# A two-layer hybrid backbone in float32: the second layer's output projection by eight plain pairs of blocks, in place of seven combined products, under a new table of ranks

## The chip, the cores and the metric

The kernel runs on one core of a Trainium2 chip. TensorE (PE) multiplies matrices, VectorE (DVE), ScalarE (ACT) and GpSimd (POOL) work element by element, and SyncE (SP) issues the DMAs. The metric is the device time of one launch in microseconds; the time quoted is the median of three runs.

## The reference

Latent tokens `x` (1024 tokens of width 1024) and context tokens (256 of the same width) pass through two layers. In float32, each layer does:

```python
hx = rms_norm(x, g_mix[i]) * (1.0 + sc1) + sh1
zx = hx @ w_in[i]                                  # 1024 -> 1280 columns: q, k, v, pool, fourier
mx = jnp.concatenate([latent_attention(q, k, v, kc, vc),       # 512 columns
                      pool_mix(...), fourier_mix(...)], -1)    # 256 + 256 columns
x = x + ga1 * (mx @ w_out[i])                      # the output projection, 1024 x 1024
fx = rms_norm(x, g_ffn[i]) * (1.0 + sc2) + sh2
x = x + ga2 * swiglu(fx, w_gate_up[i], w_down[i])  # 1024 -> 2 x 2816 -> 1024
```

The context goes through the same steps in the first layer. In the second layer it only gives keys and values, and `x` alone is returned.

## The kernel before, in words

Everything is kept transposed: features on the 128 partitions, tokens along the free axis. The latent tokens are two chunks, A (token offset 256, 512 tokens) and B (offset 768, 512 tokens); a width of 1024 is eight blocks of 128 features, called k as an input and ct as an output.

A float32 product is made of three matmuls. Each operand is written as a high part, rounded to the format that TensorE takes at full rate, and a low part, the rest: one cast (`hi`) and one subtraction (`lo`), in `halve` (L1730). `mm3` (L483) then issues low by high, high by low and high by high, on L485, L486 and L487. So one 128x128 block of weights times 512 tokens is three matmuls of 128x512.

The output projection of both chunks is a 2 by 2 by 2 block product: w_out in four quarters of 512x512, and the mixers' output in four tiles (chunk A or B, k 0 to 3 or k 4 to 7; k 0 to 3 are the attention's heads, k 4 to 7 the pool and Fourier parts). Before, it is done by seven combined products (Strassen's scheme, table `SEVEN`). Each product has 4 output blocks of 4 inputs, times 3 matmuls. Its two operands are sums or differences of quarters and of tiles: `block` (L1854) loads a half row of a quarter and the operation named `out sum` adds two of them; `summed` (L1742) adds two tiles of the mixers' output into a scratch page `ws` (`mix sum`). Both are then split by `halve` (`out hi`, `out lo`, `mix hi`, `mix lo`). Each finished accumulator `ps_o` is added to `x`, scaled, by `add_to` (L1879), in one or two places: 12 places times 4 blocks, 48 additions (named `residual`, L1883). The products come in the order 5, 7, 1, 2, 4, 3, 6; chunk A is complete after the fifth, chunk B after the seventh.

`finish_x` (L1868) then stores the chunk and runs its norm (`normed`, L1758): squares on ACT, their sums on DVE, a matmul that adds over partitions (L699), root, reciprocal, a matmul that spreads the result (L708), eight scalings on DVE (L1765), eight shifts on ACT, and the operands of the next combined products: A0 and DA from chunk A alone; B1, DB, S1, S7, S6 with chunk B.

In the second layer the FFN starts with five early units (`EARLIES`, L376), each a pair of products that needs only A0 and DA; then come units that need DB and B1, S1, S7 and S6. FFN weights may be loaded only once `second_pass` has begun, the first matmul of the seventh product (L1917).

SBUF is cut into named pages of 4 KB per partition (`H`, `W`, `MIX`, `RES`, `C`, `ST`). The attention uses `H[768][:4]`, `H[256][:4]`, `C`, `RES[0]` and `b6` for its softmax pages; the page `ws` is taken from `C[2:]` after the attention's last value products.

No instruction order is written out by hand. Each piece of work is an operation of a `Plan` with its cost, its predecessors, the pages and PSUM banks it takes, and a rank. `Plan.run` simulates the engines and issues, at each step, the ready operation that can start first, by rank among those close together. The rank is the place in the program plus an entry of `SHIFTS` by name and layer; the entries reach some 4 ms either way, so they act as priorities. `ENGINES` says for each name which of ACT (A), DVE (D) and POOL (G) may do it, and the planner chooses among them. TensorE's own products stay in program order. Names in the attention: `Z` scales a softmax page of 1024 columns, `Y` one of 256, `C` copies transposed blocks out of PSUM, `O` copies a finished head out of PSUM.

The few lines that order the projection:

```python
Y_ORDER, Y_FINAL = (5, 7, 1, 2, 4, 3, 6), {256: 4, 768: 6}
...
        for n, p in enumerate(Y_ORDER):
            blocks, how, to = SEVEN[p]
            for two in (0, 2):
...
                    e = seven(dst, w, yop[p], [AREAS] * (q == two), gate if n == 0 and q < 2 else ())
```

Of the kernel before, what the change touches and what calls it, by code (L numbers as in the profile page):

```python
# [13 lines left out]
ALU = mybir.AluOpType  # L14
# [5 lines left out]
KT = D_MODEL // P  # L20
# [256 lines left out]
def setting(table, name, default):  # L277
# [13 lines left out]
ENGINES = {"C": "AD", "G": "G", "H": "ADG", "O": "A", "Y": "AD", "Z": "ADG", "act hi": "A", "act lo": "DG", "act sum": "D",  # L291
# [6 lines left out]
           "mix sum": "DG", "norm hi": "ADG", "norm lo": "G", "norm shift": "ADG", "out hi": "A", "out lo": "DG",  # L298
# [4 lines left out]

SHIFTS = ({"C": 919100, "EC": -545700, "EL": -1073100, "MC": -4100900, "ML": 314500, "N": -759500, "O": -2444400,
           "R": -2036600, "SA": 235500, "SB": -740400, "SC": -579700, "T": -221600, "V": -416700, "Y": 278400,
           "Z": 895000, "aa": -841600, "act hi": -1263600, "act lo": -1492900, "act sum": 1970600, "ada": -662600,
# [65 lines left out]

Y_ORDER, Y_FINAL = (5, 7, 1, 2, 4, 3, 6), {256: 4, 768: 6}
Y_RANK, LEAD_Y = 0, 20000
CT_GATE = 5
EARLIES = (2, 2), (5, 0)  # L376

STARTS = (((0, 0), (0, 1), (1, 0), (1, 1)), ((0, None), (1, None)))
# [2118 lines left out]
```

## Time and profile before

| what | us |
|---|---|
| median of 3 runs (2601.51 to 2606.92) | 2603.08 |
| the profiled execution, its own time | 2608.01 |
| its span | 2605.9 |
| TensorE busy in the span | 2531.5 |
| VectorE busy | 2091.2 |
| ScalarE busy | 1253.5 |
| GpSimd busy | 540.2 |

A busy TensorE is counted from the start of a matmul to a modelled end, and matmuls overlap: the time between two starts is shorter than one matmul's duration. "Idle before, releaser" tells how long an engine waited and which instruction ended the wait. The second layer's projection lies at about 1860 to 1952 us of the span, the first layer's at 480 to 620.

### The profile page before, as it was taken

The page shows a single profiled execution, that of the slowest core. Times are in us where ns is not written, and L with a number is a line of the kernel's source. Part 1 is how long each engine was busy: PE and PEld are TensorE (multiplying, and loading weights), DVE is VectorE, ACT ScalarE, POOL GpSimd, SP SyncE. Part 2 cuts the span into 40 slices and gives each one's busy share as a digit, 9 for nine tenths or more (in the row PEclk, how much of TensorE's full clock was granted, in tenths as well). Part 3 has the DMA queues.
Part 4 walks back from the last instruction along what each step waited for, and adds up shares of the span by engine and source line. Part 5 has one row for each costly group of instructions (what it writes and reads, how often), then busy time and mean ns, then how long its engine had stood idle before and what let it go on. Part 6 is the DMA issues. An engine that isn't in the chain of part 4 may idle for free.

```text
span 2605.9 us, 38612 instructions
## 1 busy us (share of the span) xinstructions
PE 2531.5 (97%) x14382; PEld 2092.5 (80%) x14382; DVE 2091.2 (80%) x3466; ACT 1253.5 (48%) x2319; POOL 540.2 (21%) x450
## 2 busy tenths in 40 slices
PE   6999999998999999999999999999998999999999
PEld 5887777787788888888888988777776888888887
DVE  6766877799866998876788987877799977777886
ACT  4324888746322222224444533899746333334442
POOL 2022222122200000000223313322132311111241
PEclk9999999999999999999999999999998999999999
DMA  8243200354224455448434333100352423225733
GB/s 296 84 130 109 75 1 1 114 182 131 96 91 146 154 164 169 145 156 291 148 97 125 105 93 101 39 1 1 99 183 87 158 107 115 81 98 213 231 95 124
DMA packets 126203, 314.83 MB, mean 121 GB/s; under 512 B 14784, under 2 KB 23360, under 8 KB 126016
## 3 DMA queue, kind: packets, MB, share of 16 engines
q1 hardware_dynamic: 126016, 312.36, 36.4%
q8 instruction: 114, 1.87, 0.3%
q14 instruction: 73, 0.60, 0.1%
HBM read 244.94 MB, written 62.13 MB: 118 GB/s over the span
## 4 chain that ended last, share of the span: by engine, by line
PE 78%; DVE 14%; ACT 3%; DMA 2%; issue 2%; POOL 0%; SPq 0%; DVEq 0%; ACTq 0%; POOLq 0%
PE ps_s L485 8%; PE ps_s L486 8%; PE ps_s L487 8%; PE ps_d L485 6%; PE ps_d L486 6%; PE ps_d L487 6%; PE ps_pv L1512 5%; PE ps_t L1488 4%; PE ps_s L1537 4%; DVE half L475 3%; PE ps_in L485 3%; PE ps_in L486 3%; PE ps_in L487 3%; DVE x L1883 2%; DVE ws L475 1%
## 5 line engine op out<-in xcount | busy, mean ns | idle before, releaser
L472 ACT CAST half<-ws 128x512 fp32r<-128x512 f32 x404 | 243.9, 620 | 524.0 <-PE ps_s L487 236.6
L486 PE MATMUL ps_s<-half 128*128 128x512 f32 x1056 | 413.8, 392 | 6.4 <-DVE half L475 6.4
L485 PE MATMUL ps_s<-half 128*128 128x512 f32 x1056 | 414.8, 393 | 3.2 <-ACT half L472 2.6
L487 PE MATMUL ps_s<-half 128*128 128x512 f32 x1056 | 412.5, 391 | 0.0
L485 PE MATMUL ps_d<-half 128*128 128x512 f32 (+1 forms) x792 | 290.7, 367 | 2.0 <-ACT half L472 2.0
L486 PE MATMUL ps_d<-half 128*128 128x512 f32 (+1 forms) x792 | 290.2, 366 | 0.5 <-DVE half L475 0.5
L487 PE MATMUL ps_d<-half 128*128 128x512 f32 (+1 forms) x792 | 290.1, 366 | 0.0
L475 DVE TENSOR_TENSOR half<-ws,half 128x512 fp32r<-128x512 f32 x354 | 243.2, 706 | 56.6 <-ACT half L472 55.2
L486 PEld LDWEIGHTS ps_s<-half 128*128 128x128 f32 x1056 | 199.4, 189 | 50.7 <-DVE half L475 9.0
L485 PEld LDWEIGHTS ps_s<-half 128*128 128x128 f32 x1056 | 199.2, 189 | 46.6 <-ACT half L472 3.4
L487 PEld LDWEIGHTS ps_s<-half 128*128 128x128 f32 x1056 | 199.4, 189 | 41.6
L472 ACT CAST half<-wst 128x512 fp32r<-128x512 f32 x224 | 132.6, 618 | 163.9 <-PE ps_s L487 82.8
L475 POOL TENSOR_TENSOR ws<-wst 128x512 f32<-128x512 f32 x72 | 107.2, 1489 | 500.2 <-DVE half L475 413.8
L475 DVE TENSOR_TENSOR ws<-wst 128x512 f32<-128x512 f32 x258 | 173.4, 689 | 9.6 <-DMA wst<-in_w_gate_up 4.9
L475 DVE TENSOR_TENSOR half<-wst,half 128x512 fp32r<-128x512 f32 x204 | 152.3, 770 | 35.8 <-ACT half L472 35.6
L485 PEld LDWEIGHTS ps_d<-half 128*128 128x128 f32 x792 | 150.1, 190 | 26.7 <-ACT half L472 2.4
L486 PEld LDWEIGHTS ps_d<-half 128*128 128x128 f32 x792 | 150.1, 190 | 24.8 <-DVE half L475 0.7
L475 POOL TENSOR_TENSOR half<-ws,half 128x512 fp32r<-128x512 f32 x56 | 76.5, 1365 | 449.8 <-ACT half L472 396.2
L487 PEld LDWEIGHTS ps_d<-half 128*128 128x128 f32 x792 | 150.0, 189 | 24.0
L1450 DVE TENSOR_REDUCE smalls<-ps_s 128x1 f32<-128x1024 f32 x128 | 153.9, 1213 | 10.1 <-PE ps_s L1537 10.0
L485 PE MATMUL ps_in<-parts,w 128*128 128x512 f32 (+1 forms) x416 | 158.8, 382 | 1.6 <-ACT parts L472 1.6
L1512 PE MATMUL ps_pv<-pt,v 128*64 128x256 f32 x1312 | 156.4, 384 | 0.0
(284 smaller groups left out, 5874.0 us busy)
## 6 DMA issues: line engine op xcount, KB each, us to landing
wst<-in_w_gate_up SPq DMA_DIRECT2D x99, 512.0 KB, 4.3
ast<-in_w_ada SPq DMA_DIRECT2D x96, 512.0 KB, 3.7
as<-act_spill SPq DMA_DIRECT2D x165, 256.0 KB, 2.7
hs<-in_w_out SPq DMA_DIRECT2D x96, 256.0 KB, 3.0
act_spill<-c SPq DMA_DIRECT2D x44, 512.0 KB, 4.1
wst<-in_w_down SPq DMA_DIRECT2D x44, 512.0 KB, 6.4
x_spill<-x SPq DMA_DIRECT2D x28, 512.0 KB, 3.1
x<-x_spill SPq DMA_DIRECT2D x26, 512.0 KB, 6.5
```

The lines of the kernel that those rows point to most:

```text
L472: (nc.scalar.copy if e == "A" else nc.vector.tensor_copy)(out, x)
L475: (nc.vector if e == "D" else nc.gpsimd).tensor_tensor(out, x, y, op)
L485: nc.tensor.matmul(o, wl, xh, start=start, stop=False)
L486: nc.tensor.matmul(o, wh, xl, start=False, stop=False)
L487: nc.tensor.matmul(o, wh, xh, start=False, stop=stop)
L1450: nc.vector.tensor_reduce(self.pair.col(1, self.h), self.s, AX.X, ALU.max)
L1488: nc.tensor.transpose(self.t[:, 2 * q + h, :], src, ident)
L1512: nc.tensor.matmul(self.bank[own], v[:, own], self.pt[k0][:, g, 2 * P * q:2 * P * q + 2 * P], start=(k0 + q == 0), stop=(k0 + q == self.nk ...
L1537: nc.tensor.matmul(o, self.q[0][:, self.h0 + h, :], kv["k", k0](self.g, j), start=(j == 1), stop=(j == 0))
L1883: nc.vector.scalar_tensor_tensor(v, o(), s, v, ALU.mult, ALU.add)
```

## The change

The second layer alone (`DIRECT = (False, True)`) computes its projection directly. The sixteen tiles of the mixers' output (two chunks, eight k) are each split once into high and low parts, without sums. w_out is loaded by output block: eight loads of 512 KB, each split into two halves by `Feed.add` (operations `load yout`, `hi yout`, `lo yout`); the split weights stay in their pages from chunk A's use until chunk B's. The work goes by pairs of output blocks, in the order A0 A1 A2 B0 A3 B1 B2 B3 (the digit is the pair): per block eight inputs of three matmuls, k 4 to 7 first. Each accumulator is added to `x` in one place. Chunk A is complete after the fifth pair, chunk B after the eighth, and `second_pass` is the first matmul of pair B1. The first two weight blocks go into `W`; the others wait for the attention's last value products and have `W`, `c0`, `c1`, `b8`, `b9`, `a8`, `a9` and `H[0]` as rooms. The pages of the mixers' tiles (`H[256]`, `H[768]`) are freed at the last matmul of pair A3 and of pair B3.

The tables `ENGINES` and `SHIFTS` are replaced for both layers: nearly every rank differs, and many names may run on other engines. `hi yout` is not in the table and falls under `hi*`.

```diff
--- before
+++ after
-ENGINES = {"C": "AD", "G": "G", "H": "ADG", "O": "A", "Y": "AD", "Z": "ADG", "act hi": "A", "act lo": "DG", "act sum": "D",
-           "eh": "D", "el": "DG", "f copy": "AD", "gate": "DG", "hi dft": "ADG", "hi dftc": "G", "hi in0": "AG",
-           "hi in1": "ADG", "hi in2": "AD", "hi in3": "D", "hi in4": "A", "hi in5": "DG", "hi in6": "A",
-           "hi in7": "ADG", "hi in8": "AD", "hi in9": "DG", "hi out": "ADG", "hi*": "A", "k across": "DG",
-           "k hi": "ADG", "k lo": "G", "lo dft": "D", "lo dftc": "DG", "lo in0": "D", "lo in1": "D", "lo in2": "G",
-           "lo in3": "D", "lo in4": "DG", "lo in5": "G", "lo in6": "DG", "lo in7": "D", "lo in8": "DG",
-           "lo in9": "G", "lo out": "DG", "lo*": "DG", "mix copy": "A", "mix hi": "A", "mix lo": "D",
-           "mix sum": "DG", "norm hi": "ADG", "norm lo": "G", "norm shift": "ADG", "out hi": "A", "out lo": "DG",
-           "out sum": "D", "pool hi": "AD", "pool lo": "DG", "q hi": "D", "q lo": "G", "rope add": "D",
-           "rope cos": "D", "rope sin": "DG", "square": "A", "sum": "D", "u hi": "ADG", "u lo": "DG", "v copy": "A",
-           "v hi": "A", "v out": "AD", "w hi": "A", "w lo": "DG", "w sum": "DG", "x hi": "ADG", "x lo": "D",
+ENGINES = {"C": "AD", "G": "G", "H": "ADG", "O": "D", "Y": "ADG", "Z": "D", "act hi": "A", "act lo": "DG", "act sum": "D",
+           "eh": "AD", "el": "DG", "f copy": "A", "gate": "D", "hi dft": "A", "hi dftc": "ADG", "hi in0": "AD",
+           "hi in1": "G", "hi in2": "ADG", "hi in3": "AG", "hi in4": "AG", "hi in5": "AD", "hi in6": "AG",
+           "hi in7": "D", "hi in8": "ADG", "hi in9": "A", "hi out": "ADG", "hi*": "A", "k across": "A",
+           "k hi": "ADG", "k lo": "G", "lo dft": "D", "lo dftc": "DG", "lo in0": "DG", "lo in1": "G", "lo in2": "D",
+           "lo in3": "G", "lo in4": "DG", "lo in5": "G", "lo in6": "G", "lo in7": "DG", "lo in8": "D", "lo in9": "G",
+           "lo out": "DG", "lo yout": "D", "lo*": "DG", "mix copy": "A", "mix hi": "AD", "mix lo": "DG",
+           "mix sum": "DG", "norm hi": "ADG", "norm lo": "D", "norm shift": "ADG", "out hi": "A", "out lo": "DG",
+           "out sum": "DG", "pool hi": "ADG", "pool lo": "DG", "q hi": "D", "q lo": "DG", "rope add": "D",
+           "rope cos": "DG", "rope sin": "G", "square": "A", "sum": "DG", "u hi": "AG", "u lo": "DG", "v copy": "AD",
+           "v hi": "A", "v out": "AD", "w hi": "A", "w lo": "DG", "w sum": "DG", "x hi": "A", "x lo": "D",
            "x shift": "A", "x sum": "DG"}
 
 
-SHIFTS = ({"C": 919100, "EC": -545700, "EL": -1073100, "MC": -4100900, "ML": 314500, "N": -759500, "O": -2444400,
...
+SHIFTS = ({"C": 114200, "EC": -631900, "EL": -874800, "MC": -1126400, "ML": -33800, "N": -2136800, "O": 342200, "R": -480200,
...
@@ -373,6 +373,9 @@
+DIRECT = (False, True)
+Y_PAIRS = ([(256, 0), (768, 0), (256, 1), (768, 1), (256, 2), (768, 2), (256, 3), (768, 3)], [(256, 0), (256, 1), (256, 2), (768, 0), (256, 3), (768, 1), (768, 2), (768, 3)])
@@ -1807,27 +1810,36 @@
+        if DIRECT[l]:
+            for ch, h, pages in ((A, 1, H[256][4:]), (B, 1, H[768][4:]), (A, 0, H[256][:4]), (B, 0, H[768][:4])):
+                for kk in range(4):
+                    k = 4 * h + kk
+                    b = yop[ch, k] = Box()
+                    halve(b, lambda ch=ch, k=k: col(mix, ch, k), mixed(ch, k), (pages[kk],), plan.t + Y_RANK, "mix")
+                    yuse[ch, k // 2] += b.ready
+        else:
...
@@ -1837,9 +1849,10 @@
+        if not DIRECT[l]:
+            less.op = op("D", 100, negate, [mod_op[l, GA1 * KT], mod_op[l, GA1 * KT + 4]], rank=plan.t - 20000, name="negate")
...
-        for n, pages in enumerate((ST, C[:2])):
+        for n, pages in enumerate(() if DIRECT[l] else (ST, C[:2])):
@@ -1887,41 +1900,76 @@
+        if DIRECT[l]:
+            wt, room_y = {}, W + ("c0", "c1") + (("b8", "b9", "a8", "a9") + tuple(H[0]) if last else ())
+            begun_y = False
+            for ch, two in Y_PAIRS[l]:
                 o, first = Box(), None
-                for q in (two, two + 1):
-                    rank = plan.t - LEAD_Y
-                    w = Box()
-                    stage = stages[n in (2, 4, 6)]
-                    sts = [block(l, q, i_, j_, stage, rank) for i_, j_ in blocks]
-                    dep = [s.op for s in sts]
-                    if how is not None:
-                        dep = [op("sum", 512, lambda e, a=sts[0], b=sts[1], how=how: combine(e, a.t, a.t, b.t, how), dep, give=[sts[1].op],
-                                  rank=rank, name="out sum")]
-                    halve(w, lambda a=sts[0]: a.t, dep, W, rank, "out", order=[h_turn])
-                    h_turn = w.op
-                    join(w.ready, [sts[0].op])
-                    stage[2].extend(w.ready)
+                for q in range(2):
+                    ct = 2 * two + q
+                    if ct not in wt:
+                        late = len(wt) >= 2
+                        wt[ct] = feed.add(i["w_out"][l, ct], room_y if late else W, plan.t - LEAD_Y, uses["v"][0][-8:] if late else (), "yout")
+                        h_turn = wt[ct][1].op
                     def dst(*tag, o=o, q=q):
                         if tag:
                             o.t = bank(tag[0], [2, 512], "ps_o")
-                        return o.t[:, q % 2, :]
+                        return o.t[:, q, :]
                     start = len(plan.ops)
-                    e = seven(dst, w, yop[p], [AREAS] * (q == two), gate if n == 0 and q < 2 else ())
+                    e = product(dst, wt[ct], lambda k, ch=ch: [yop[ch, k].t[:, j, :] for j in range(2)],
+                                lambda k, ch=ch: yop[ch, k].ready, 512, () if begun_y else gate, [AREAS] * (q == 0),
+                                ks=(4, 5, 6, 7, 0, 1, 2, 3))
+                    begun_y = True
                     first = first or plan.ops[start]
-                    if n == 6 and q == 0:
+                    if ch == B:
+                        join([e], [h.op for h in wt[ct]])
+                    if (ch, ct) == (B, 2):
                         second_pass = first
-                    join([e], [w.op])
-                join([add_to(ch, q + 4 * z, sign, lambda o=o, q=q: o.t[:, q % 2, :], e, None)
-                      for q in (two, two + 1) for ch, z, sign in to], [first])
-            join([e], [b.op for b in yop[p]])
-            for ch in (A, B):
-                if p == Y_FINAL[ch]:
+                    a = add_to(ch, ct, 1, lambda o=o, q=q: o.t[:, q, :], e, None)
+                    added = [a] if q == 0 else added + [a]
+                join(added, [first])
+                if two == 3:
+                    join([e], [yop[ch, k].op for k in range(KT)])
                     finish_x(ch)
...
```

## Rows read from the trace of the kernel before

**Rows 1.** The profile's page: the span, and its first part, busy time of each engine with its share of the span and its instruction count.

```profile
span 2605.9 us, 38612 instructions
...
PE 2531.5 (97%) x14382; PEld 2092.5 (80%) x14382; DVE 2091.2 (80%) x3466; ACT 1253.5 (48%) x2319; POOL 540.2 (21%) x450
```

**Rows 2.** Busy time by stage. Columns: the stretch, its length, busy us (and instructions) of TensorE's matmuls, its weight loads, VectorE, ScalarE and GpSimd, the granted TensorE clock as a share of full speed, the DMA engines' share, GB/s. The stretches are the kernel's beginning, the end of the first layer's projection with the norm behind it, the attention of the second layer, and the second layer's projection and what follows it.

```profile
0.00:60.00 60.00, 38.88 (x427) 29.12 (x428) 38.21 (x70) 26.17 (x36) 12.33 (x17) 1.00 0.85 315
575.00:640.00 65.00, 54.90 (x334) 48.57 (x333) 62.95 (x112) 40.81 (x66) 19.67 (x20) 0.95 0.51 162
1630.00:1866.00 236.00, 231.06 (x1669) 178.49 (x1668) 182.79 (x363) 220.71 (x451) 59.31 (x63) 1.00 0.07 21
1866.00:1955.00 89.00, 84.59 (x387) 67.16 (x385) 83.06 (x127) 40.63 (x63) 26.42 (x19) 0.96 0.55 178
1955.00:2010.00 55.00, 44.77 (x183) 35.88 (x184) 53.97 (x87) 37.10 (x58) 8.86 (x7) 0.90 0.22 71
```

**Rows 3.** TensorE in order of time inside the second layer's projection, where it never waits: start us, duration us, instruction. These are the first and the last of 148 lines.

```profile
1905.20 0.39 PE L487 MATMUL ps_o<-half 128*128 128x512 f32 x1
...
1938.52 0.39 PE L487 MATMUL ps_o<-half 128*128 128x512 f32 x1
```

**Rows 4.** The same stretch of the second layer, from the first matmul of its projection to the last, and from there until TensorE no longer waits; columns as in rows 2.

```profile
1859.80:1952.30 92.50, 89.40 (x419) 71.90 (x418) 82.95 (x126) 42.98 (x68) 26.42 (x19) 0.96 0.51 165
1952.30:2013.00 60.70, 49.16 (x197) 38.77 (x196) 58.01 (x93) 37.65 (x58) 11.34 (x7) 0.89 0.26 82
```

**Rows 5.** The same columns for the instructions that read or write one accumulator alone: first the projection's `ps_o` in the first of these two stretches, then the FFN's `ps_s` and `ps_m` in the second.

```profile
1859.80:1952.30 92.50, 81.26 (x336) 64.32 (x336) 31.48 (x46) 0.96 0.51 165
...
1952.30:2013.00 60.70, 43.00 (x167) 33.08 (x168) 0.00 (x0) 6.01 (x6) 0.89 0.26 82
...
1952.30:2013.00 60.70, 2.88 (x12) 2.25 (x12) 0.00 (x0) 0.89 0.26 82
```

**Rows 6.** Who TensorE waited for between 1860 and 2013 us: total us, times, longest us.

```profile
PE ps_s L486 <- DVE half L475: 5.7, 5, 3.4
PE ps_ss L699 <- DVE sq L690: 4.7, 1, 4.7
PE ps_o L486 <- DVE half L475: 2.8, 2, 1.8
```

**Rows 7.** Ten microseconds of the projection after its first long wait; columns as in rows 2.

```profile
1880.00:1890.00 10.00, 7.23 (x20) 5.35 (x20) 8.93 (x15) 3.37 (x6) 0.93 (x1) 0.66 0.20 58
```

**Rows 8.** Groups of instructions between 1866 and 1955 us on VectorE, ScalarE and GpSimd: line, engine, operation, tiles, count, then busy us and mean ns of one, then the engine's idle time before them.

```profile
L1883 DVE SCALAR_TENSOR_TENSOR x<-ps_o,mod,x 128x512 f32<-128x512 f32 x40 | 27.9, 740 | 0.9 <-PE ps_o L487 0.9
...
L475 DVE TENSOR_TENSOR half<-ws,half 128x512 fp32r<-128x512 f32 x21 | 15.0, 715 | 1.5 <-ACT half L472 1.5
...
L475 DVE TENSOR_TENSOR ws<-mix 128x512 f32<-128x512 f32 x15 | 10.3, 691 | 0.5
L475 DVE TENSOR_TENSOR hs<-hs 128x512 f32<-128x512 f32 x13 | 8.9, 682 | 1.3 <-DMA hs<-in_w_out 1.3
...
L475 DVE TENSOR_TENSOR half<-hs,half 128x512 fp32r<-128x512 f32 x11 | 7.6, 689 | 0.1
...
L1883 DVE SCALAR_TENSOR_TENSOR x<-ps_o,negs,x 128x512 f32<-128x512 f32 x8 | 6.0, 744 | 0.2 <-PE ps_o L487 0.2
```

**Rows 9.** The instructions that read the mixers' output `mix`, from 1745 us on: count, shortest, median and longest ns, first and last start.

```profile
L475 DVE TENSOR_TENSOR ws<-mix x15: 683/692/693, 1869.6 to 1922.9; 128x512 f32<-128x512 f32 x15
...
L475 DVE TENSOR_TENSOR half<-mix,half x4: 678/680/684, 1766.1 to 1805.8; 128x512 fp32r<-128x512 f32 x4
```

**Rows 10.** VectorE in order of time around the two halves' norms: start us, duration us, instruction, count.

```profile
1929.17 2.71 DVE L1883 SCALAR_TENSOR_TENSOR x<-ps_o,mod,x 128x512 f32<-128x512 f32 x4
...
1944.76 1.28 DVE L1765 TENSOR_TENSOR x<-x,ps_rs 128x512 f32<-128x512 f32 x2
...
1953.01 1.40 DVE L1883 SCALAR_TENSOR_TENSOR x<-ps_o,mod,x 128x512 f32<-128x512 f32 x2
...
1957.29 2.47 DVE L1765 TENSOR_TENSOR x<-x,ps_rs 128x512 f32<-128x512 f32 x4
...
1967.16 0.68 DVE L1765 TENSOR_TENSOR x<-x,ps_rs 128x512 f32<-128x512 f32 x1
```

**Rows 11.** Groups of instructions in the second layer's attention, 1630 to 1866 us, columns as in rows 8. `p` and `pt` are the softmax's exponentials and their transposes.

```profile
L472 DVE COPY pt<-ps_t 128x512 f32<-128x512 f32 x74 | 49.8, 683 | 14.0 <-PE ps_t L1488 14.0
L472 ACT COPY pt<-ps_t 128x512 f32<-128x512 f32 x84 | 47.9, 589 | 5.3 <-PE ps_t L1488 5.1
...
L1475 POOL TENSOR_SCALAR p<-p,smalls 128x1024 f32<-128x1024 f32 x31 | 35.8, 1154 | 128.6 <-ACT pt L472 75.0 <-PE ps_s L1537 44.8 <-DVE smalls L1555 5.3
L1473 ACT ACTIVATE p<-p,smalls 128x1024 f32<-128x1024 f32 x30 | 34.3, 1144 | 0.0
...
L472 ACT COPY mix<-ps_pv 128x256 f32<-128x256 f32 x15 | 5.6, 376 | 0.0
...
L1475 DVE TENSOR_SCALAR p<-p,smalls 128x1024 f32<-128x1024 f32 x3 | 2.2, 745 | 0.0
```

**Rows 12.** The weight conversions of both layers' projections: shortest, median and longest ns of one on VectorE and on GpSimd.

```profile
L475 DVE TENSOR_TENSOR half<-hs,half x32: 672/683/1156, 279.2 to 1933.5; 128x512 fp32r<-128x512 f32 x32
L475 POOL TENSOR_TENSOR half<-hs,half x24: 1269/1300/2134, 493.5 to 1941.1; 128x512 fp32r<-128x512 f32 x24
```

**Rows 13.** The profile's sixth part, DMA issues: out<-in, queue, operation, count, KB each, median us from issue to landing.

```profile
wst<-in_w_gate_up SPq DMA_DIRECT2D x99, 512.0 KB, 4.3
```

More of the change, by code (lines that the diff above doesn't have):

```diff
@@ new lines, in layer @@
+        if DIRECT[l]:
[6 more added lines that the diff above has]
+        else:
+            YP = [(5, H[256][4:], ((B, 1),), None), (7, H[768][4:], ((A, 1), (B, 1)), ALU.add),
+                  (1, H[256][:4], ((A, 0), (B, 1)), ALU.add), (2, H[768][:4], ((A, 0),), None),
+                  (4, H[256][4:], ((A, 1), (A, 0)), ALU.subtract), (3, H[768][4:], ((B, 0), (B, 1)), ALU.subtract),
+                  (6, H[256][:4], ((A, 0), (B, 0)), ALU.add)]
+            y_turn = None
+            for p, pages, tiles, how in YP:
+                yop[p] = [Box() for _ in range(4)]
+                for kk in range(4):
+                    ts = [(ch, 4 * h + kk) for ch, h in tiles]
+                    src_ = [lambda ch=ch, k=k: col(mix, ch, k) for ch, k in ts]
+                    deps = [d for ch, k in ts for d in mixed(ch, k)]
+                    if how is None:
+                        halve(yop[p][kk], src_[0], deps, (pages[kk],), plan.t + Y_RANK, "mix")
+                        done = yop[p][kk].ready
+                    else:
+                        y_turn = summed(yop[p][kk], *src_, how, deps, (pages[kk],), plan.t + Y_RANK, "mix", tuple(sums_slots[:2]), order=[y_turn])
+                        done = [y_turn]
+                    for ch, k in ts:
+                        yuse[ch, k // 2] += done
@@ L1921, in layer, with dst @@
-            join([e], [b.op for b in yop[p]])
-            for ch in (A, B):
-                if p == Y_FINAL[ch]:
-                    finish_x(ch)
+                    a = add_to(ch, ct, 1, lambda o=o, q=q: o.t[:, q, :], e, None)
[3 more added lines that the diff above has]
+                    join([e], [yop[ch, k].op for k in range(KT)])
+                    finish_x(ch)
+        else:
+            for n, p in enumerate(Y_ORDER):
+                blocks, how, to = SEVEN[p]
+                for two in (0, 2):
+                    o, first = Box(), None
+                    for q in (two, two + 1):
+                        rank = plan.t - LEAD_Y
+                        w = Box()
+                        stage = stages[n in (2, 4, 6)]
+                        sts = [block(l, q, i_, j_, stage, rank) for i_, j_ in blocks]
+                        dep = [s.op for s in sts]
+                        if how is not None:
+                            dep = [op("sum", 512, lambda e, a=sts[0], b=sts[1], how=how: combine(e, a.t, a.t, b.t, how), dep, give=[sts[1].op],
+                                      rank=rank, name="out sum")]
+                        halve(w, lambda a=sts[0]: a.t, dep, W, rank, "out", order=[h_turn])
+                        h_turn = w.op
+                        join(w.ready, [sts[0].op])
+                        stage[2].extend(w.ready)
+                        def dst(*tag, o=o, q=q):
+                            if tag:
+                                o.t = bank(tag[0], [2, 512], "ps_o")
+                            return o.t[:, q % 2, :]
+                        start = len(plan.ops)
+                        e = seven(dst, w, yop[p], [AREAS] * (q == two), gate if n == 0 and q < 2 else ())
+                        first = first or plan.ops[start]
+                        if n == 6 and q == 0:
+                            second_pass = first
+                        join([e], [w.op])
+                    join([add_to(ch, q + 4 * z, sign, lambda o=o, q=q: o.t[:, q % 2, :], e, None)
+                          for q in (two, two + 1) for ch, z, sign in to], [first])
+                join([e], [b.op for b in yop[p]])
+                for ch in (A, B):
+                    if p == Y_FINAL[ch]:
+                        finish_x(ch)
```

93 lines of the change are left out of this document (36 added, 57 removed), and 44 rows, old and new, of the table SHIFTS.

## The prediction

> **What bounds the kernel now.** I read the page's first part, then busy time by stage, then who TensorE waited for in the stage that changes. TensorE is busy 2531.5 of 2605.9 us [rows 1], so all its waiting is 74 us, and 21 of them lie in the first 60 us, before operands exist [rows 2]. Any gain must come from waits and from stretches at the lower clock; any added matmul is paid in full. In the second layer's projection and behind it VectorE is full: 83.06 of 89 us, then 53.97 of 55 [rows 2], and every long wait of TensorE there ends on VectorE or on the norm that VectorE feeds [rows 6]. So TensorE bounds the kernel nearly everywhere, and VectorE bounds this stage.
>
> **TensorE's added work.** Seven products x 4 blocks x 4 inputs x 3 = 336 matmuls, as the accumulator's row has them [rows 5]. Direct: 2 chunks x 8 blocks x 8 inputs x 3 = 384. Where TensorE never waits, 148 lines start within 33.32 us, so one costs 33.32/147 = 0.2267 us [rows 3]. 48 more cost **+10.9 us**, with nothing to hide them.
>
> **VectorE's removed work.** Gone are 20 sums of weight quarters and 20 of mixers' tiles (0.68 and 0.69 us), 12 of 28 weight splits and 12 of 28 tile splits, and 32 of 48 residual additions. The 48 additions took 27.9 + 6.0 = 33.9 us in this window, 0.71 each; the sums and splits beside them 15.0 + 10.3 + 8.9 + 7.6 = 41.8 [rows 8]. What stays is 16 additions (11.3), 16 weight splits (11) and at most 16 tile splits (11): 33 for 75.7 us. VectorE has room again, and the projection becomes TensorE's. ScalarE loses 24 casts; it was busy 40.63 of 89 us [rows 2], so that is worth nothing.
>
> **The first wait.** Before, product 7 ran out of operands: TensorE waited 2.8 us for a VectorE split [rows 6], and the next ten microseconds were granted a mean clock of 0.66, between the levels of 1.2 and 2.4 GHz, while TensorE was busy 7.23 us [rows 7]: 0.34 x 7.23 = 2.5 us more. The cause is in the code: the tile sums need the scratch page that is freed after the attention's last value product, and the first sum starts at 1869.6, while plain splits of the same `mix` ran at 1766.1 to 1805.8, inside the attention [rows 9]. The direct form has only plain splits, so both are ready before the first pair. **-5.3 us.** Late next are the third and fourth weight blocks, which wait for the attention's last value product. The nearest load of 512 KB lands in 4.3 us [rows 13], cast and subtraction add 1.3; pair A0 covers it with 48 x 0.2267 = 10.9 us. I cost it at nothing, at 3 us if that cover is short. There are 8 loads where there were 48, so SP's queue gets shorter.
>
> **From the projection's end to full speed.** Before: 60.7 us from 1952.3 to 2013, with 58.01 us of VectorE work [rows 4]; it holds 167 + 12 matmuls of the FFN [rows 5], with two left of the projection 181 of 512 columns: 181 x 0.2267 = 41.0 us; the other 16 of its 197 instructions are the norm's. A's last additions came at 1929.17 + 2.71 = 1931.9, its scalings from 1944.76 until 1959.8, beyond the projection's end; B's last additions ended at 1954.4, its scalings began at 1967.16 [rows 10]. After: A is complete after 5 of 8 pairs, 240 matmuls, just as before after 5 of 7 products, but 144 matmuls (32.6 us) follow it instead of 96 (21.8). A's chain took 1959.8 - 1931.9 = 28 us on a full VectorE; its squares still wait for pages that pair A3 frees, but with VectorE at half load it fits into 32.6. So the five early units start without a wait. Of VectorE's 58.0 us some 9.5 are A's (four scalings, four sums, eight splits at 0.6 to 0.7), and some 7 are early units' weights, which may now be made earlier, since `second_pass` starts 32 us before the projection's end and not 11. That leaves 41.5 for VectorE, beside 41.0 + 1.9 for TensorE (the 16, estimated at half a long one's cost each). Two engines so evenly loaded don't overlap perfectly: I keep the 5.7 us of waits on splits [rows 6] and take 42.9 + 5.7 = 48.6, **-12.1 us**. Bounds: 42.9 (-17.8) and 60.7 (0).
>
> **The rest of the kernel.** Every rank and many engine sets are new, and no row shows what a planner makes of them. Below, the bound is the waiting that exists: the second layer's attention idles 4.9 us, the first layer's stretch after its projection 10.1 us and a clock of 0.95 with VectorE busy 62.95 of 65 [rows 2]. There `mix lo`, `out sum` and the norm's `sum` may now go to GpSimd too, which was busy 19.67 of 65. I take **-2 us** for it, nearer to zero than to its 10.1 + 2.7, since GpSimd needs about twice VectorE's time for one (1300 against 683 ns [rows 12]). For the attention I take 0: there `Z` and `O` go to VectorE alone. 31 `Z` on GpSimd and 30 on ScalarE become 61 x 0.745 = 45.4 us, and 15 `O` at VectorE's rate for a copy out of PSUM (683 ns for 512 columns, so 0.34 each) 5.1 [rows 11]. VectorE would stand at 182.8 + 50.5 = 233.3 of 236 us, if nothing left it; ScalarE loses 34.3 + 5.6 = 39.9 of 220.7. `C` may go to either, 74 of them now on VectorE; moving 35 gives 209 and 201 us. It fits, with little to spare.
>
> **Sum.** 10.9 - 5.3 - 12.1 - 2 = -8.5 us, on the profiled execution's 2608.0 (its span and 2.1 us around it): 2599.5. That execution is 4.9 us above the median, so against the median 2603.1: **2594.6**.
>
> **The rivals.**
> *B's chain sets the end anyway.* From B's last addition to full speed was 2013 - 1954.4 = 58.6 us. If that chain keeps its length, since the sums for S1, S7 and S6 all need B, the end moves with B: 10.9 - 5.3 = +5.6, 2608.7. For it: VectorE full throughout. Against it: 16 us of that work were A's and the early units'.
> *The attention becomes VectorE's.* This one is slower. Each layer's 236 us hold 233.3 us of VectorE work unless `C` moves; GpSimd keeps 59.3 - 35.8 = 23.5 us and gets some of `Y`. If the two also exclude each other, 256.8 us must fit into 236: +20.8 per layer at worst, +41.6 if the first layer's is like it. With half of the `C` shift made (17 of 35, 11.6 us), +9.2 per layer: 2594.6 + 18.4 = 2613. It decides from the point where VectorE and GpSimd together pass TensorE's 231 us. That they hold each other up is seen in pairs of like splits: longest 1156 against 683 ns on VectorE, 2134 against 1300 on GpSimd [rows 12]; against it, `C` can move 35 times where 17 already halve the overload. The Trainium skill ("SBUF — State Buffer", section "SBUF: two separate sides") says that a VectorE instruction in a two-port mode, or one with two SBUF inputs, and a GpSimd instruction that reads SBUF take a shared pair of ports as an exclusive lock for their whole length. By that rule the 20.8 us per layer stand if no `C` moves.
> *More is returned elsewhere.* Some 38 us of waits lie outside this stage and the first 60 us: 74.4 - 21.1 - 4.4 - 10.2 [rows 1, 2]. If the new ranks take a third of them, 13 us: 2582. For it: many sets are wider. Against it: only 10.1 of the 38 lie together.
> *No change in sum.* The stage gains 6.5 and the rest loses as much, since names such as `hi in1`, `lo in1` and `rope sin` may now run on GpSimd alone: 2603.
>
> **How the numbers follow.** Chances: forecast 0.42, B's chain 0.12, attention 0.13, more elsewhere 0.18, no change 0.15. About 0.2%, 5.2 us, is what a measurement can tell from no change. Faster: the forecast but for its upper quarter (0.32) and "more elsewhere" (0.18), 0.50. Same: that quarter (0.10), no change (0.15) and a little of B's chain (0.02), 0.27. Slower: the rest of B's chain and the attention, 0.23. The range goes from 2578 (more elsewhere, a little beyond) to 2612 (just short of the attention case); the forecast's own is 2588 to 2601: its largest term alone goes 12.1 up and 5.7 down, of which I keep about half above and all below.
>
> **What would show it.** Right: 384 matmuls into `ps_o`, no wait of TensorE on a split between its first and last one; the projection's stretch at about 92.5 + 10.9 - 5.3 = 98 us; the early units start at once behind it; about 49 us from there to full speed; VectorE near half busy in the projection; both attentions as long as before. Wrong: attentions longer by microseconds with VectorE over 95% busy; a gap at pair A1 for weights; waits at the norm's L699 or L708; or the stage as forecast and the sum elsewhere.

## The result and the profile after

The changed kernel takes 2636.29 us (median of 4 runs, 2632.74 to 2637.66) against 2602.77 of the kernel before on the same chip: the medians lie 33.5 us apart, and the ratio of the runs is 1.0117, with a 95% interval of 1.0105 to 1.0129. Forecast were 2594.6 us, with a range that ended at 2612. The profiled execution took 2632.74 us, 3.6 below its median; its page answers to [rows 1]:

```profile
span 2631.0 us, 38495 instructions
...
PE 2548.8 (97%) x14430; PEld 2101.5 (80%) x14430; DVE 2116.4 (80%) x3460; ACT 1208.5 (46%) x2244; POOL 484.1 (18%) x410
```

TensorE has its 48 added matmuls, ScalarE and GpSimd lost 45 and 56 us, and VectorE, which was to lose work, has 25 us more. Where the time went is read from the starts of the first and last matmul into each stage's accumulator. All columns are us. "Start" runs to the end of the first layer's projection, "FFN" from there to its first down product; the down products (277 to 280 us everywhere) stand between FFN and the next column. "QKV and attention" is the second layer's, up to the projection's first matmul, "behind" runs from the projection to the FFN's last `ps_s`, and some 215 us follow it. The stages of a row are those of one execution. The later rows are the experiments below.

| kernel | median | start | FFN | QKV and attention | projection | behind |
|---|---|---|---|---|---|---|
| before | 2602.8 | 618.9 | 585.7 | 376.6 | 92.2 | 439.1 |
| after | 2636.3 | 620.1 | 585.2 | 388.4 | 114.6 | 429.3 |
| e1, tables alone | 2648.3 | 620.8 | 587.7 | 405.6 | 96.2 | 441.1 |
| e3, late additions | 2631.3 | 623.8 | 589.1 | 388.5 | 105.9 | 431.7 |
| e7, and other pair order | 2623.8 | 624.4 | 585.1 | 388.6 | 100.0 | 431.8 |
| e5, before with three engine sets | 2639.7 | 620.7 | 609.6 | 382.8 | 95.7 | 438.7 |
| e6, after with the sets of before | 2670.2 | 628.2 | 599.8 | 407.1 | 110.0 | 431.1 |
| e2, direct, old tables | 2617.1 | 614.2 | 583.3 | 385.9 | 107.6 | 430.3 |
| e4, and late additions | 2614.0 | 616.6 | 585.3 | 385.9 | 96.2 | 433.4 |
| e8, refitted | 2602.5 | 615.9 | 583.4 | 379.5 | 96.3 | 431.9 |
| e9, refitted otherwise | 2604.2 | 616.3 | 584.0 | 378.7 | 96.2 | 433.6 |
| e10, e8 with early additions | 2617.6 | 615.2 | 584.0 | 380.1 | 106.6 | 435.9 |

The median of e9 counts one execution of its twelve that took 5100.36 us; that of the other eleven is 2603.26.

The first layer is in sum as long as before, within what executions of one plan differ by: up to the second layer's projection the changed kernel, e3 and e7 are planned alike, and their "start" goes from 620.1 to 624.4. The spans differ by 25.1 us: 0.7 in start and FFN, +11.8 in the second QKV and attention, +22.4 in the projection, -9.8 behind it. (The medians differ by 33.5, since before's profiled execution was 5 us above its median and this one 3.6 below.) Busy time by stage of the changed kernel, columns as in [rows 2], for the attention, the projection and the stretch until TensorE no longer waits:

```profile
1645.10:1872.40 227.30, 220.44 (x1558) 163.00 (x1556) 208.82 (x399) 172.47 (x370) 30.09 (x46) 0.99 0.02 6
1872.40:1987.40 115.00, 104.93 (x496) 81.88 (x495) 48.32 (x75) 34.82 (x55) 2.87 (x2) 0.99 0.30 104
1987.40:2040.00 52.60, 47.54 (x204) 37.69 (x204) 48.71 (x70) 33.57 (x52) 7.63 (x5) 0.97 0.21 70
```

In the projection VectorE is down from 82.95 us [rows 4] to 48.32, as reckoned, and the stretch is still 22.5 us longer. Who TensorE waited for from 1872 to 2040 us says why (total, times, longest):

```profile
PE ps_o L488 <- DVE x L1896: 5.9, 7, 0.8
...
PE ps_o L488 <- DVE w L478: 3.3, 1, 3.3
```

Neither wait is in [rows 6]. The first is on the residual addition, the second on the splits of a weight block. In order of time, TensorE and then VectorE, at one of the first one's seven places:

```profile
1942.47 0.39 PE L489 MATMUL ps_o<-half,w 128*128 128x512 f32 x1
1942.70 0.39 PE L490 MATMUL ps_o<-half,w 128*128 128x512 f32 x1
1943.93 0.50 PE L488 MATMUL ps_o<-half,w 128*128 128x512 f32 x1 [0.84 <-DVE x L1896]
1944.27 0.40 PE L489 MATMUL ps_o<-half,w 128*128 128x512 f32 x1
```

```profile
1943.13 0.75 DVE L1896 SCALAR_TENSOR_TENSOR x<-ps_o,mod,x 128x512 f32<-128x512 f32 x1 [6.05 <-PE ps_o L490]
```

The matmul at 1943.93 begins the second block of a pair, 1.23 us behind the one before it instead of 0.23: it starts when VectorE's addition of the *first* block ends (1943.13 + 0.75 = 1943.88). It writes the other half of the tile, so no data ask for this; both halves are one tile `o`, and the addition now stands between the two products.

In the attention TensorE's listed waits come to 6.1 us, against 3.0 before. The attention goes by quads, pieces of work that each end in a long group of value products; a quad's length is the time from one such group to the next. The 14 quads between the first long group and the fifteenth, before and then after, columns as in [rows 2]:

```profile
1657.20:1853.40 196.20, 196.20 (x1459) 151.51 (x1458) 151.02 (x302) 189.58 (x390) 49.13 (x51) 1.00 0.02 5
```

```profile
1661.90:1867.50 205.60, 203.32 (x1453) 149.95 (x1452) 188.65 (x363) 156.36 (x334) 22.81 (x39) 1.00 0.01 4
```

TensorE's matmuls look 100 and 99% busy, with six fewer in 9.4 us more after. The weight loads beside them give it away: 151.51 / 196.20 = 77% busy before, 149.95 / 205.60 = 73% after. The Trainium skill ("Perfetto Trace Analysis", section "Identifying the Most-Contended Engine") says that matmul busy time is no measure of nearness to the limit, because matmuls are pipelined, and weight-load busy time is one; the two rows bear it out. Who ScalarE waited for shows the lost time plainly, before (1641.7 to 1859.9) and after (1645.1 to 1872.4):

```profile
ACT pc L1460 <- DVE smalls L1454: 1.5, 5, 0.8
ACT pd L1460 <- DVE smalls L1454: 1.0, 6, 0.2
```

```profile
ACT pc L1463 <- DVE smalls L1457: 20.0, 12, 1.8
ACT pd L1463 <- DVE smalls L1457: 13.5, 12, 1.8
```

The exponentials stand 33.5 us behind VectorE's `smalls`, the rows' negated maxima; before it was 2.5. A quad took 14.01 or 14.02 us before, always; after it takes 13.7 to 15.7, 14.69 on average. Of the 11.8 us that QKV and attention are longer, these quads are 9.4 and the time ahead of the first of them 4.0; the projection begins 1.6 sooner behind the last, with 93 of the attention's transposes and value products still to come in its stretch, against 65 before. So a part of the attention's price stands in the projection's column.

### The profile page after: what moved, and what is told of

Same layout as the page of the kernel before. It is cut to its first block, busy times and chain, and to the rows that moved or that the text cites. A ratio compares the mean times of both kernels' runs of the same rounds, so it can differ in the third digit from the quotient of the medians.

```text
span 2631.0 us, 38495 instructions
## 1 busy us (share of the span) xinstructions
PE 2548.8 (97%) x14430; PEld 2101.5 (80%) x14430; DVE 2116.4 (80%) x3460; ACT 1208.5 (46%) x2244; POOL 484.1 (18%) x410
## 4 chain that ended last, share of the span: by engine, by line
PE 81%; DVE 13%; ACT 2%; DMA 2%; issue 1%; SPq 0%; DVEq 0%; ACTq 0%
PE ps_s L488 9%; PE ps_s L489 9%; PE ps_s L490 9%; PE ps_d L489 6%; PE ps_d L488 6%; PE ps_d L490 6%; PE ps_pv L1515 4%; PE ps_t L1491 4%; PE ps_s L1540 3%; PE ps_in L488 3%; PE ps_in L489 3%; PE ps_in L490 3%; DVE half L478 2%; DVE smalls L1453 2%; PE ps_c L488 2%; PE ps_c L489 2%
## 5 line engine op out<-in xcount | busy, mean ns | idle before, releaser
L475 ACT CAST half<-ws 128x512 fp32r<-128x512 f32 x390 | 235.2, 620 | 498.5 <-PE ps_s L490 240.2
L478 DVE TENSOR_TENSOR half<-ws,half 128x512 fp32r<-128x512 f32 x333 | 234.8, 710 | 59.3 <-ACT half L475 57.7
L478 DVE TENSOR_TENSOR ws<-wst 128x512 f32<-128x512 f32 x274 | 205.6, 753 | 14.8 <-DMA wst<-in_w_gate_up 6.4
L478 POOL TENSOR_TENSOR ws<-wst 128x512 f32<-128x512 f32 x56 | 79.9, 1428 | 540.4 <-DVE half L478 393.3
L478 POOL TENSOR_TENSOR half<-ws,half 128x512 fp32r<-128x512 f32 x57 | 82.3, 1443 | 470.8 <-ACT half L475 470.8
L1469 ACT ACTIVATE p<-ps_s,smalls,rq 128x1024 f32<-128x1024 f32 x128 | 154.5, 1209 | 0.0
```

The source lines that it names most:

```text
L475: (nc.scalar.copy if e == "A" else nc.vector.tensor_copy)(out, x)
L478: (nc.vector if e == "D" else nc.gpsimd).tensor_tensor(out, x, y, op)
L1469: nc.scalar.activation(self.p, self.s, AF.Exp, bias=pr.col(2, h), scale=rq[pr.at][:, h:h + 1], accum_out=pr.col(4, h))
```

## The experiments

My theory after this reading: the new tables cost the attention's time, the direct form the projection's, by a false wait and late weights. Rivals: the tables are harmless and the direct form's operands slow the attention; or the tables are to blame for all; or it is VectorE's larger share by the three sets `O`, `Y`, `Z`.

**e1, the tables alone.** Seven products in both layers under the new tables.

```diff
-DIRECT = (False, True)
+DIRECT = (False, False)
```

> The changed kernel's rank and engine tables with the seven combined products in both layers, so the direct form alone is taken out. My theory: of the 33.5 us lost, the tables cost about 14 in the second layer's attention (a quad of rows takes 14.69 us in place of 14.02, 14 quads, and it starts 4.7 late) and the direct projection the other 19 to 20. Then this kernel stands near 2602.8 + 14 = 2617 (2611 to 2623), its second attention still at 14.5 us or more a quad. Rival 1, the direct form alone is to blame, the attention's slower pace being a matter of what the projection's early operands take there: 2603 (2599 to 2607) and 14.0 us a quad. Rival 2, the tables are to blame for all of it: 2636 (2630 to 2642).

Measured: 2648.3, ratio 1.0179 (1.0163 to 1.0195). Worse than the whole change and longer than any of the three cases allowed; the nearest is the rival that blames the tables for everything. QKV and attention take 405.6 us, the projection 96.2, behind it 441.1. ScalarE waits for the maxima even longer:

```profile
ACT pd L1464 <- DVE smalls L1458: 24.1, 14, 2.8
ACT pc L1464 <- DVE smalls L1458: 20.5, 15, 2.3
```

So under the new tables the direct form *saves* 12 us (2648.3 to 2636.3): 17.2 in QKV and attention and 11.8 behind, against 18.4 in the projection. Why the attention gains isn't shown: the seven products' tile sums don't run in it (the first starts at 1913.0, the projection at 1894.2), and VectorE's work in the fourteen quads is the same, 189.11 us here and 188.65 in the changed kernel. It is no fair price of the seven products, though: the second layer's new ranks have no entries for the names that only they use, and these got the first layer's.

**e5 and e6, the engine sets.** Three sets of the change put into the kernel before, and taken out of the change; all ranks stay.

```diff
-... "O": "A", "Y": "AD", "Z": "ADG", ...
+... "O": "D", "Y": "ADG", "Z": "D", ...
```

> The kernel before, its ranks untouched, with three entries of the engine table changed as the change has them: the softmax's scaling and the mixers' copy on VectorE alone, the exponentials' sums on all three engines. My theory: this makes the second layer's attention VectorE's, 14.02 us a quad becoming 14.6 to 14.9, so 8 to 13 us there and up to as much in the first layer: 2612 (2608 to 2625). Rival: the engine sets are harmless, and the slower pace comes of the new ranks' order: 2603 (2600 to 2606), 14.0 us a quad.

> The changed kernel with those three entries put back as they were before: the scaling free on all three engines, the mixers' copy on ScalarE. My theory: VectorE's share in the second layer's attention falls from 92% and the pace returns to about 14.0 us a quad: 2636 - 9 to 14 = 2624 (2621 to 2628). Rival (ranks' order): the pace stays at 14.5 or more and the time at 2636 (2632 to 2642).

Measured: e5 2639.7, ratio 1.0136 (1.0114 to 1.0158); e6 2670.2, ratio 1.0262 (1.0245 to 1.0278). Each is longer than its theory and its rival allowed. That e5 is slower is what my theory said, and it deceives, since the pace is not where it lost the time. The 14 quads of e5 and then of e6:

```profile
1686.70:1883.70 197.00, 197.00 (x1461) 151.30 (x1460) 180.16 (x350) 161.84 (x348) 29.67 (x49) 1.00 0.02 5
```

```profile
1685.10:1906.60 221.50, 203.53 (x1457) 151.46 (x1456) 170.90 (x342) 185.40 (x373) 25.62 (x23) 0.99 0.01 3
```

Who the exponentials waited for in these attentions, e5 (1669.6 to 1890.2) and e6 (1669.0 to 1914.1):

```profile
ACT pd L1460 <- DVE smalls L1454: 1.4, 3, 0.5
ACT pc L1460 <- DVE smalls L1454: 0.7, 1, 0.7
```

```profile
ACT pd L1463 <- DVE smalls L1457: 15.0, 8, 2.4
```

With the old ranks VectorE is 180.16 / 197.00 = 91% busy, about as in the changed kernel (188.65 / 205.60 = 92%), and a quad takes 14.07 us; the exponentials hardly wait. (The text before e2's run says 14.16: it took a window that ends 1.3 us behind the fifteenth group.) With the new tables and the old three sets (e6) VectorE is 77% busy, and a quad takes 15.8. So a full VectorE alone doesn't slow the attention, and the attention is slow without one: what the new tables bring is an order in which, above all, maxima come late. Two things stay open. The ranks weren't parted from the other new engine sets: `q lo`, for one, was GpSimd's alone, and under the new set 12 of these splits, 5.6 us, are among VectorE's 188.65. And that work would be 96% of the 196.2 us that the quads took before; no run shows VectorE that full at that pace. For the ranks speaks that the first layer's attention, under the same engine sets and ranks of its own, keeps its pace (14.9 us a quad for 15.0).

Of the 33.4 us by which e5's span is longer, 23.9 lie in the first layer's FFN, which uses none of the three sets. Two stretches of it, in e5 and then in the kernel before:

```profile
740.00:860.00 120.00, 116.82 (x698) 97.91 (x696) 72.64 (x112) 33.72 (x58) 6.30 (x4) 0.97 0.33 110
860.00:980.00 120.00, 113.50 (x595) 97.24 (x594) 109.07 (x168) 29.71 (x52) 6.45 (x4) 0.96 0.44 145
```

```profile
740.00:860.00 120.00, 119.40 (x749) 101.08 (x748) 80.74 (x127) 33.33 (x58) 9.01 (x7) 1.00 0.43 138
860.00:980.00 120.00, 119.50 (x645) 103.36 (x644) 112.09 (x169) 34.61 (x59) 12.05 (x8) 1.00 0.46 148
```

TensorE gets through 101 fewer matmuls in these 240 us, and in the whole FFN it waits for VectorE's splits:

```profile
PE ps_s L485 <- DVE half L475: 11.3, 6, 3.2
```

The orders of the two kernels part at about 250 us, in the first layer's attention, at a scaling of a softmax page, which `Z` allots. My reading, not tested further, is that ranks which fitted the old plan no longer fit once it has shifted, and that the price then falls where it happens to.

**e3, the false wait.** Both additions of a pair issued after both products.

```diff
-                    a = add_to(ch, ct, 1, lambda o=o, q=q: o.t[:, q, :], e, None)
-                    added = [a] if q == 0 else added + [a]
-                join(added, [first])
+                join([add_to(ch, 2 * two + q, 1, lambda o=o, q=q: o.t[:, q, :], e, None) for q in range(2)], [first])
```

> The changed kernel with both additions of a pair of blocks issued after both blocks' products, as the seven products have it. My theory: the accumulator of a pair is one tile, so the second block's first matmul waits for the first block's addition, 0.84 us by the trace and about 1.0 with the refill, in seven of eight pairs; without that wait the projection is 7 to 8 us shorter, and the time 2629 (2626 to 2632). Rival: the wait only takes the place of another (the operands' conversions or the norm behind it), and the time stays at 2636 (2634 to 2638) although the rows of 0.84 us are gone.

Measured: 2631.3, ratio 1.0111 (1.0095 to 1.0127). The projection is 8.7 us shorter and its waits on `x` are gone. The time fell by 5 only by the medians, and the two intervals overlap; in the profile the start and the FFN, planned alike, came out 7.6 longer, so this pair doesn't settle what the wait is worth to the kernel. e10 comes back to it.

**e7, the late weights.** e3 with another order of the pairs.

```diff
-... [(256, 0), (256, 1), (256, 2), (768, 0), (256, 3), (768, 1), (768, 2), (768, 3)])
+... [(256, 0), (768, 0), (256, 1), (256, 2), (256, 3), (768, 1), (768, 2), (768, 3)])
```

> The changed kernel with late additions and another order of the eight pairs: the large chunk's first pair runs second, so that the third and fourth block of the weights, whose load waits for the attention's last values, are wanted one pair (some 13 us) later. My theory: the wait of 3.3 us and the half clock behind it go, 3 to 6 us of 2631: 2625 to 2628. Rival: the large chunk's second operands are no earlier than the weights, the wait moves to them, and the time stays at 2631 or is longer.

Measured: 2623.8, a little under the expected 2625 to 2628, ratio 1.0078 (1.0061 to 1.0095). The projection, e3's and then this one:

```profile
1880.30:1986.40 106.10, 102.11 (x496) 82.20 (x494) 45.97 (x73) 33.88 (x54) 2.89 (x2) 0.98 0.33 113
```

```profile
1876.90:1977.10 100.20, 100.20 (x496) 81.19 (x495) 46.07 (x73) 33.88 (x54) 2.90 (x2) 1.00 0.34 120
```

No listed wait is left, the clock is full, 5.9 us are gone: e3's wait of 4.0 us (3.34 in the changed kernel) and matmuls at a lower clock behind it. In the changed kernel six of these come 0.43 us apart instead of 0.23, and the granted clock from 1898.2 to 1902.0 is 0.56 on average, so mostly at the lower of its two levels. In the changed kernel the weights' load was not what came late. The two loads were issued from 1873.0 on and had landed by 1882.3. The splits came late, because VectorE takes them behind chunk B's last tile casts and splits, which wait for the attention's last copy (VectorE sat idle 8.36 us before it), though B's tiles are wanted two pairs later:

```profile
1892.01 0.42 DVE L475 COPY mix<-ps_pv 128x256 f32<-128x256 f32 x1 [8.36 <-PE ps_pv L1515]
1892.35 1.09 DVE L475 CAST half<-mix 128x512 fp32r<-128x512 f32 x3
1893.35 2.98 DVE L478 TENSOR_TENSOR half<-mix,half 128x512 fp32r<-128x512 f32 x3
1896.26 0.74 DVE L1896 SCALAR_TENSOR_TENSOR x<-ps_o,mod,x 128x512 f32<-128x512 f32 x1
1896.92 2.48 DVE L478 TENSOR_TENSOR w<-wst,w 128x512 fp32r<-128x512 f32 x4
```

**e2 and e4, the direct form under the old tables.** Engine and rank tables of the kernel before, with the three names that only the direct form has, and one added order, without which the planner finds no way through. e4 has the late additions too.

```diff
-... ready[g], *kd, j=h, take=[AREAS])
+... ready[g], *kd, *([main[0]] if last and first_sa == 5 else []), j=h, take=[AREAS])
+                            first_sa += 1
```

> The direct second layer under the kernel before's engine and rank tables; only the names that the direct form is new to (its weights' load and two halves) get ranks, and one order is added so that the planner finds a way through: the sixth scores of the second attention wait for the last product before it. My theory now (the new ranks are to blame, not the direct form and not VectorE's larger share: the old ranks with the new engine sets ran the second attention at 14.16 us a quad, the new ranks with either set at 14.69 and 15.7): the pace is 14.0 to 14.2 us, the projection 114 as in the changed kernel, what follows it some 10 shorter than before. 2603 + 22 - 10 = 2615, and up to 8 more where the added order holds the attention's start back: 2615 to 2623. Rival (what the direct form takes in the attention sets its pace, whatever the ranks): 14.6 us a quad or more, 2625 to 2632.

> The one before it with both additions of a pair issued after both blocks. By my theory the projection loses 8 to 9 us as it did under the new ranks (114.6 to 105.9), some 3 of them given back behind it: 2608 to 2617. If the gain under the new ranks was chance of the plan, no change against the run beside it.

Measured: e2 2617.1, ratio 1.0062 (1.0048 to 1.0076); e4 2614.0, ratio 1.0039 (1.0026 to 1.0053). Of the change's 33.5 us, 19.2 go when the old tables return (2636.3 to 2617.1). Most of e2's quads take 13.5 to 14.6 us, two 16.05, on average 14.29, a little over the expected 14.0 to 14.2, and QKV and attention are 9.3 us longer than before: the added order's price, or the form's. The projection falls from 107.6 to 96.2 with the late additions, and TensorE waits in it no more. The time falls by only 3.1, and the two intervals overlap: in e4's profile start and FFN, planned alike, are 4.4 longer than e2's, and what follows the projection is 3.1 longer. So this pair doesn't settle the wait's worth either.

**e8 and e9, refitted.** e4 with a milder order (the third scores wait for the last product but one), the first two weight blocks loaded behind the last weights of the input products, and ten (e8) or nine (e9) other ranks of the second layer moved.

```diff
-... *([main[0]] if last and first_sa == 5 else []), ...
+... *([prods[{2: -2}[first_sa]]] if last and first_sa in {2: -2} else []), ...
...
-... uses["v"][0][-8:] if late else (), "yout")
+... uses["v"][0][-8:] if late else in_last, "yout")
```

> The direct second layer with late additions under the kernel before's tables, nearer to its plan: the third scores of the second attention wait for the last product but one (in place of the sixth for the last), the first two weight blocks are loaded only behind the last weights of the input products, and ten of the second layer's ranks are moved. My theory: what was left against the kernel before (2614 to 2602.9) is mostly the start of the second attention, 9.3 us later in the profile, and two quads of 16.05 us in it, not the direct form as such. With these gone, projection +4 and behind it -6 as measured: 2603 to 2607. Rival (the direct form costs some ten microseconds there however it is ordered): 2611 to 2616.

> The same with another set of ten moved ranks of the second layer, among them the scaling's, the exponentials' and the queries', found from another start. By the same theory 2603 to 2607; if the two sets differ by more than 3 us, the difference is the plan's alone.

Measured: e8 2602.5, ratio 0.9994 (0.9985 to 1.0002); e9 2604.2, ratio 0.9999 (0.9990 to 1.0007). e9 is within the expected 2603 to 2607, e8 half a microsecond under it; they are 1.7 us apart. The projection of e8, and its attention's waits for the maxima:

```profile
1856.00:1952.50 96.50, 96.50 (x468) 79.23 (x467) 41.62 (x63) 32.87 (x52) 3.80 (x4) 1.00 0.31 111
```

```profile
ACT pc L1465 <- DVE smalls L1459: 1.3, 6, 0.5
ACT pd L1465 <- DVE smalls L1459: 1.1, 5, 0.4
```

TensorE runs from the projection's first matmul to its last without a listed wait at full clock. Against the kernel before, QKV and attention are 2.9 us longer, the projection 4.1, what follows 7.2 shorter: nothing in sum. Since ranks were moved for the direct form and not for the seven products, this is a comparison of two fitted plans, not of the two forms alone.

**e10, the false wait in a plan without others.** e8 with the additions as the change has them (e3's diff, reversed).

> The first refitted kernel with one thing put back as the change has it: each block's addition issued right behind its own product, between the two blocks of a pair. My theory: the false wait on the pair's one accumulator tile is back, 0.84 us and the refill in seven or eight pairs, so the projection grows from 96.3 to 104 or more, and the time from 2602.5 to 2608 to 2611. Rival (what the projection gains from late additions is given back behind it): 2602 to 2605, the time between projection and first product's end 8 us shorter.

Measured: 2617.6, ratio 1.0052 (1.0036 to 1.0069), 15 us above e8 and more than the expected 2608 to 2611. The projection is 10.3 longer, and what follows 4.0. Its waits from 1850 to 2020 us:

```profile
PE ps_s L489 <- ACT half L476: 8.6, 2, 5.7
PE ps_o L489 <- DVE x L1901: 6.8, 8, 0.8
```

The second line is the false wait, in all eight pairs here. The first lies behind the projection, where e8 waits 4.7 us for the same, so nothing there gives the false wait back. In this plan the place where additions are issued is worth more than the forecast gave the whole change. In the two other pairs it took 8.7 us (e3) and 11.4 (e4) out of the projection, and 5.0 and 3.1 out of the medians with intervals that overlap: its price in the projection is shown three times, what the kernel pays for it hangs on the plan.

## Why the prediction was wrong, step by step

- **48 matmuls, +10.9; the first wait, -5.3.** Right where the plan lets them be: the projection was to take 98 us, and takes 96.2 or 96.3 in e4, e8 and e9, without a listed wait and with the clock at 1.00. In e7, also without one, it takes 100.0: under the new tables 28 more of the attention's matmuls fall into its stretch, as in the changed kernel.
- **No wait inside the projection.** First failure: a wait that the text didn't have. The addition moved in between two products that share one tile: 8.7 us of the projection's 22.4 (e3). The diff showed it; the forecast counted additions and not where they are issued.
- **Third and fourth weight blocks, nothing, or 3 us with a short cover.** Second failure: 3.34 us of wait (4.0 in e3) and the lower clock behind it, 5.9 together by e7 against e3. "A gap at pair A1 for weights" was named as a sign of error and came. Not the load was late but the splits, in VectorE's queue.
- **The attention, 0.** Third failure, and the largest single one: +11.8 in QKV and attention, and 3.8 more in the projection's stretch (e7's 100.0 against 96.2). The step compared busy times ("It fits, with little to spare"), and such a load does fit: e5 runs at 91% of VectorE with 14.07 us a quad. What the step can't see is order: under the new tables the exponentials wait 33.5 us for maxima. That the tables are the cause is shown by e2, e8 and e9, where the direct form under the old ones takes 14.06 to 14.29 us a quad; which of their entries, is not.
- **From the projection's end to full speed, -12.1.** Its mechanism held: the early units start without a gap, chunk A's scalings end at 1978.3, ahead of the projection's end and not behind it, the wait of 4.7 us at the norm's sums [rows 6] is gone, and VectorE's work in the stretch is 48.71 us for 58.01. The size: 60.7 became 52.6 with seven matmuls more in it (204 for 197), so -8.1 by that measure, -9.8 by the table, and -3.2 to -8.8 in the kernels with the direct form under the old tables.
- **The rest, -2.** Nothing came: the start 1.2 longer, the FFN 0.5 shorter.

The sum: forecast -8.5, spans +25.1. The gap of 33.6 is 11.8 (attention), 16.8 (projection, 22.4 against 5.6), 2.3 (behind) and 2.7 (rest). The projection's 22.4 add up from the experiments: 8.7 for the additions, 5.9 for the weights, 3.8 for the attention's matmuls and 4.0 (96.2 against 92.2) for the direct form without these. Against the forecast's 2594.6 the median is 41.7 off; the 8 us beyond 33.6 are the distances of the two profiled executions from their medians.

Of the rivals, "B's chain sets the end anyway" falls with -9.8 behind the projection. "The attention becomes VectorE's" had the right sign and place, but the reason that it gave, VectorE's load, is not by itself what slows e5 or e6. Nor do VectorE and GpSimd exclude each other wholly, as its 256.8 us supposed: in e5's quads they are busy 180.16 + 29.67 = 209.8 us within 197.0. The long splits of [rows 12] come of a narrower case. Of the 24 on GpSimd in the kernel before, the nine that began beside a VectorE operation reading SBUF alone took 1644 to 2134 ns; the fifteen that began beside one reading an accumulator took 1269 to 1307. In the changed kernel's quads 133.6 of VectorE's 188.65 us read accumulators, so the 20.8 us a layer would not stand even if no `C` moved. "More is returned elsewhere" found nothing (+0.7 in start and FFN), and with no gain in the stage "no change in sum" falls too.

That the stage would gain 6.5 is not confirmed either: with plans of its own the direct form is worth 0 (e8, e9). What stays open is whether a longer search finds a plan in which it is worth more. No version here beats both kernels: e8 equals the one before and is 34 us faster than the change by the medians.

## What to carry to other kernels

A rank table goes with the program that it was made for: put a new table, or one changed set, to the test by itself, and look for its cost in stages that it doesn't touch. Where an operation that reads an accumulator is moved in between two that write it, look whether both halves are one tile. Whether an engine's work fits is settled by who waits in order of time, not by its busy share; where TensorE's matmuls look fully busy, compare the weight loads' share.

## What the runs showed that I had not expected

- TensorE's matmuls were busy 196.20 of 196.20 us and 203.32 of 205.60 for almost the same work; most of the 9.4 us that it lost doesn't show as idle time of the matmuls.
- VectorE at 91% busy did not slow the attention (14.07 us a quad), 92% in another order went with a slow one (14.69), and 77% with a slower one (15.8).
- A wait of 0.84 us costs 1.0 to 1.3 us a pair in the projection (1.23 us between two starts instead of 0.23; 8.7 us for seven, 10.3 for eight); eight of them stand in a kernel that is 15 us slower (e10 against e8), because the stretch behind then waits longer as well.
